# The 1/rms row of the first SwiGLU, formed between the halves of the second gate/up pair instead of ahead of both

## The chip, the cores and the metric

The kernel runs on one core of a Trainium2 chip, as one launch. The metric is device time in microseconds (us) of that core, from runs of the whole program. The profile is one further execution of the same program, taken by the hardware profiler. Engines are named as the profile names them: PE (TensorE matmuls), PEld (its weight loads), DVE (VectorE), ACT (ScalarE), POOL (GpSimd), SP (SyncE, which issues most DMAs).

## The reference

One decoder layer on 512 tokens of width 1024, all in float32: a SwiGLU half step, a mixer with two groups of attention heads, a second SwiGLU half step, and a gated embedding. What the change touches is the first SwiGLU:

```
def rmsnorm(x, g):
    xf = x.astype(jnp.float32)
    y = xf * lax.rsqrt(jnp.mean(xf * xf, axis=-1, keepdims=True) + EPS)
    return (y * g.astype(jnp.float32)).astype(x.dtype)

def swiglu(x, wg, wu, wd):
    return (jax.nn.silu(x @ wg) * (x @ wu)) @ wd

h = h + 0.5 * swiglu(rmsnorm(h, ffn1_norm[i]), ffn1_wg[i], ffn1_wu[i], ffn1_wd[i])
```

The hidden width is 2816. 1/rms is one number per token, so it may be multiplied in before or after the products with Wg and Wu.

## The kernel before, in words

**Products.** Every float32 product is made of three matmuls: both operands are split into a rounded part `hi` and a rest `lo`, and hi x hi, hi x lo and lo x hi are added up in PSUM (`passes`, L459). A weight tile is loaded into a buffer `st` (3 of them), rounded on ACT into a buffer `hi` (4), and the rest is formed on DVE into a buffer `lo` (4), by `split` (L375).

**The first SwiGLU.** The hidden columns are worked in 11 pairs of 128-column blocks. The token axis stays in the free dimension: a gate or up product of one block is a PSUM tile of 128 hidden columns x 512 tokens, and 24 matmuls (8 blocks of the contraction x 3 passes). Pair 0 is done by `ffn_start` (L473): x arrives transposed and without 1/rms, and its four products fill two `gub` and two `acc` banks of PSUM. Pairs 1 and 2 are done by `gate_up` (L552), each as two halves (r = 0 and 1) of a gate and an up product, all in `gub` banks, of which there are four. Pairs 3 to 10 are done by `Blocks` (L1292) with a scheme of seven block products per pair; its operands on the x side, `x8_165` to `x8_170` and `k4_171`/`k4_172` in the listings below, are built by `x_operands` (L581) from four `pt` buffers, which the scheme's first weights then reuse. Some of these weights are sums that a DMA of POOL's queue adds into a `pt` buffer (`accum_op`), others sums made on DVE (`V.tensor_add`). `down` (L618) multiplies the hidden values with Wd.

**The row.** Because x has no 1/rms in it, every product of pairs 0 to 2 and every operand of `x_operands` is multiplied by a row: 1/rms of the 512 tokens, the same on all 128 partitions. `rms_rows` (L514) makes it. For each of four blocks of 128 tokens:

```
            nc.scalar.activation(junk, h[t], AF.Square, accum_out=ss)
            r = self.rstd(ss, D)
            rb = self.w2()[:, :P]
            nc.vector.tensor_copy(rb, r.to_broadcast([P, P]))
            nc.tensor.transpose(ps[:, t * P:(t + 1) * P], rb, self.ident)
```

that is, a square with a sum on ACT, two small operations on POOL (`rstd`, L391), a copy on DVE and a transpose on PE; then ACT copies the PSUM tile into the row. `hidden` (L529) multiplies a pair's products by the row on DVE, which also frees their PSUM banks, and applies silu on ACT and a product on DVE.

**What sets the order.** Every instruction is first recorded in program order with an estimated cost (`Plan`, L59). `issue` (L214) then replays the recording as a simulation: it takes, for each engine, the earliest operation that can start, among a window of 440 operations after the oldest one not yet placed, with buffers given out in order. What comes out is emitted as each engine's fixed order. So code that is recorded in another order can give other orders on every engine. The recorded costs and the window are the same before and after.

Of the kernel before, what the change touches and what calls it, by code (L numbers as in the profile page):

```python
# [308 lines left out]
class Layer:  # L309
# [239 lines left out]
        nc.vector.tensor_sub(lo, a, hi.bitcast(F32))  # L549
        return hi, lo  # L550

    def gate_up(self, p, xT, quarters, ahead=None):  # L552

        nc = self.nc
        out = []
        for r in range(2):
            pair = []
            for g in range(2):
                w = self.st()
                for c in range(2):  # L560
                    nc.sync.dma_start(w[:, 512 * c:512 * c + 512], quarters[p, r, c, :, 512 * g:512 * g + 512])
                w = self.split(w.rearrange("p (k c) -> p k c", k=NK), NK, P)
                if ahead and r == g == 1:
                    ahead()
                ps = self.gub()
                for k in range(NK):
                    for i, (a, b) in enumerate(self.passes(w, [y[:, k % 2] for y in xT[k // 2]])):
                        nc.tensor.matmul(ps, lhsT=a[:, k, :], rhs=b, start=(k == 0 and i == 0),
                                         stop=(k == NK - 1 and i == 2))
                pair.append(ps)  # L570
            out.append(pair)
        return out


# [71 lines left out]
                if half == 1 and final:  # L646
                    on_token(t)

    def ffn(self, h, xT, quarters, wd, on_token, started=None, row=None):


        n = FF // (2 * P)
        classic = CLASSIC + (started is not None)
        raw, acts = [], []
        blocks = Blocks(self, range(classic, n), quarters)

        def parts():
            while raw:
                acts.append(self.hidden_parts(raw.pop(0)))
        X = None  # L660
        for p in range(n):
            if p < classic:
                first = p == classic - 1
                if first:
                    blocks.ahead(7, 0, 0)
                products = started if p == 0 and started else self.gate_up(
                    p, xT, quarters, (lambda: blocks.ahead(7, 3, 2)) if first else None)
                raw.append(self.hidden(products, row))
                if p == classic - 2:
                    X = self.x_operands(xT, row)  # L670
            else:
                i = 7 * (p - classic)
                end = i + 7 if p in (3, 7, n - 1) else len(blocks.seq)
                for j in range(7):
                    blocks.ahead(i + j + 7, min(i + j + 5, end), min(i + j + 3, end))
                    if j == 2:
                        parts()
                    blocks.product(i + j, X)
                raw.append(blocks.acts)
            if p in (3, 7, n - 1):  # L680
                parts()
                e = 7 * (p + 1 - classic)
                self.down(h, acts, p + 1 - len(acts), p == n - 1, wd, on_token, lambda: blocks.ahead(e + 7, e + 3, e + 2))
                acts = []
# [69 lines left out]
    def head_norm(self, E, src, dst, gain):  # L754
# [7 lines left out]
        else:  # L762
            E.tensor_tensor(sq, src, src, ALU.mult)
        nc.vector.tensor_reduce(ss, sq, axis=AX.X, op=ALU.add)
        r = self.rstd(ss, 64, n)
# [212 lines left out]
    def cmp_attention(self, A, t, g, o):  # L978
# [10 lines left out]
        m, rs = self.small(4), self.small(4)  # L989
        nc.vector.tensor_reduce(m, s, axis=AX.X, op=ALU.max)  # L990
        bc = lambda x: x[:, :, None].to_broadcast([P, 4, 32])
        nc.gpsimd.tensor_tensor(s, s, bc(m), ALU.subtract)
        nc.scalar.activation(s, s, AF.Exp)
        nc.vector.tensor_reduce(rs, s, axis=AX.X, op=ALU.add)
        nc.vector.reciprocal(rs, rs)
# [74 lines left out]
    def mix(self, xT, rs_in, o_nsa, o_fox, nsa_out):  # L1070
# [25 lines left out]
        def kv_project():  # L1096
# [4 lines left out]
            def kv_done(t, ps):  # L1101
# [8 lines left out]
                nc.scalar.activation(sq.rearrange("p (a h d) -> p a h d", a=2, h=2), uv[:, :, 0], AF.Square)  # L1110
                V.tensor_reduce(ss, sq.rearrange("p (n d) -> p n d", n=4), axis=AX.X, op=ALU.add)
                r = self.rstd(ss, 64, 4).rearrange("p (a h) -> p a h", a=2)
# [179 lines left out]
class Blocks:  # L1292
# [4 lines left out]
    def __init__(self, layer, pairs, quarters):  # L1297
        self.layer, self.quarters = layer, quarters
        self.seq = [(p, i) for p in pairs for i in self.ORDER]
        self.sums = self.loads = self.splits = 0  # L1300
        self.src, self.w = {}, {}

    def ahead(self, sums, loads, splits):

        L = self.layer
        nc = L.nc
        V, f = nc.vector, self.src

        def load(p, name, r, c, t):
            nc.sync.dma_start(t, self.quarters[p, r, c])  # L1310
            f[p, name] = t
        while self.sums < min(sums, len(self.seq)):
            p, i = self.seq[self.sums]
            if i in (7, 5):
                load(p, i, 1, 0, L.pt().bitcast(F32)[:, :1024])
                nc.gpsimd.dma_start(f[p, i], self.quarters[p, 0, 0] if i == 7 else self.quarters[p, 1, 1],
                                    accum_op=ALU.add)
            self.sums += 1
        while self.splits < min(splits, len(self.seq)):
            self.load_to(max(loads, self.splits + 1), load)  # L1320
            p, i = self.seq[self.splits]
            src = f[p, {6: 5, 3: 5}.get(i, i)]
            if i in (6, 3):
                V.tensor_add(src, src, f[p, 1 if i == 6 else 2])
            hi, lo = L.hi(), L.lo()
            nc.scalar.copy(hi, src)
            V.tensor_sub(lo, src, hi.bitcast(F32))
            self.w[p, i] = hi, lo
            self.splits += 1
        self.load_to(loads, load)  # L1330
# [53 lines left out]
def layer(ctx, tc, d, out, upto=99):  # L1384
    L = Layer(ctx, tc, d)
# [5 lines left out]
        nc.sync.dma_start(out[0, t * P:(t + 1) * P], h[t])  # L1391
    h = [L.k4() for t in range(NT)]
    xT, started = L.ffn_start(x, h, L.gcol["ffn1_norm"], d["first"])
    row = L.rms_rows(h)
    spill = [L.dram.tile([P, D], F32, name=f"spill{t}") for t in range(NT)]
    aT, a_r = [], []

    def to_mix(t):
# [3 lines left out]
            aT.append(L.new_xT())  # L1402
        a_r.append(L.norm_tok(t, h[t], None, aT[0], L.gcol["mix_norm"]))
        nc.sync.dma_start(spill[t], h[t])
    L.ffn(h, xT, d["quarters1"], d["ffn1_wd"][0], to_mix, started, row)
    if upto == 1:
        return nc.issue()
    L.mix_consts()
# [2 lines left out]
    h = []  # L1411
# [34 lines left out]
    xT = L.pairs_xT()  # L1446
# [108 lines left out]
```

## Time and profile before

| what | value |
|---|---|
| time, median of 3 runs | 1085.66 us (1085.31 to 1086.53) |
| the profiled execution, its own time | 1086.66 us |
| its span, first to last instruction | 1084.8 us |
| PE busy | 1068.4 us, 98% of the span |
| PEld, DVE, ACT, POOL busy | 89%, 71%, 53%, 17% |
| TensorE clock granted, mean | 1.000 |

The profiled execution lies 1.00 us above the median of the runs, and its span is 1.86 us shorter than its own time. All times inside the program are us from the span's start. The busy share of PE is high because matmuls overlap one another; what matters for this change is the first 100 us, and there what PE, ACT and DVE wait for. All helpers record their operations through one line (L306), so rows are told apart by their tiles: `gub` and `acc` are PSUM, `k` the 4 KB buffers (x, the x operands of pairs 0 to 2, hidden values), `w` the 2 KB ones (the row, the copies of 1/rms, the scaled products), `s` single columns.

### The profile page before, as it was taken

To read this page: it belongs to the slowest core of one execution; us is meant where nothing else is said; L and a number is where in the kernel's file an instruction comes from. 1 tells how busy PE (TensorE), PEld (TensorE's weight loads), DVE (VectorE), ACT (ScalarE), POOL (GpSimd) and SP (SyncE) were. 2 spreads that over 40 slices of the span, in tenths; PEclk is the share of its full clock that TensorE was granted. 3 is DMA by queue.
4 is the path that set the end of the run, shared out by engine and by line. 5 is a ranking of instruction groups with operands and counts; after the bars stand their busy time and mean duration, and the time that the engine had idled before them with its cause. 6 is when DMAs were issued, how large, how long until landed. Compare 5 with 4: busy or idle time off the path is not lost.

```text
span 1084.8 us, 17688 instructions
## 1 busy us (share of the span) xinstructions
PE 1068.4 (98%) x6721; PEld 962.8 (89%) x6721; DVE 768.4 (71%) x1320; ACT 580.2 (53%) x1116; POOL 184.2 (17%) x313
## 2 busy tenths in 40 slices
PE   9999999999999999999999999999999999999998
PEld 6789899988997878999999888889989998899887
DVE  5886378744774777989889786977537784487473
ACT  5544145522543768988888864645315552255352
POOL 0010000000000246554344610310000000000000
PEclk9999999999999999999999999999999999999999
DMA  8396356643444622302102241686535674333421
GB/s 280 125 232 200 97 136 184 189 130 100 118 110 131 216 70 73 86 7 60 43 18 75 76 158 52 220 222 170 173 97 145 185 185 130 103 109 120 153 109 66
DMA packets 76532, 139.79 MB, mean 129 GB/s; under 512 B 13744, under 2 KB 33712, under 8 KB 76192
## 3 DMA queue, kind: packets, MB, share of 16 engines
q1 hardware_dynamic: 71376, 120.76, 34.4%
q0 software_dynamic: 4928, 17.89, 9.4%
q8 instruction: 53, 0.87, 0.3%
q14 instruction: 31, 0.25, 0.1%
q10 hardware_dynamic: 144, 0.02, 0.0%
HBM read 132.23 MB, written 6.42 MB: 128 GB/s over the span
## 4 chain that ended last, share of the span: by engine, by line
PE 86%; DVE 4%; ACT 3%; POOL 3%; DMA 2%; issue 2%; SPq 0%; ACTq 0%; POOLq 0%; DVEq 0%
PE acc L306 53%; PE gub L306 33%; DVE k L306 1%; POOL s L306 1%; DVE lo L306 1%; ACT w L306 1%; DMA st<-in_quarters 1%; DMA st<-in_first 1%; POOL r L306 1%; ACT k L306 1%; POOL w L306 1%; DVE w L306 1%; DMA gq<-in_q_norm_nsa 1%; ACT hi L306 1%; SPq L306 0%
## 5 line engine op out<-in xcount | busy, mean ns | idle before, releaser
L306 PE MATMUL acc<-hi,k 128*128 128x512 f32 (+1 forms) x832 | 262.7, 389 | 1.5 <-ACT k L306 0.9
L306 ACT CAST hi<-st 128x1024 fp32r<-128x1024 f32 (+4 forms) x150 | 148.5, 991 | 179.7 <-PE acc L306 93.2
L306 DVE TENSOR_TENSOR lo<-st,hi 128x1024 fp32r<-128x1024 f32 (+4 forms) x150 | 172.2, 1150 | 65.6 <-ACT hi L306 65.2
L306 PE MATMUL acc<-hi,x 128*128 128x384 f32 (+3 forms) x720 | 199.5, 349 | 0.3 <-ACT hi L306 0.3
L306 PEld LDWEIGHTS acc<-hi,k 128*128 128x128 f32 x832 | 155.9, 188 | 32.6 <-ACT k L306 1.8
L306 PE MATMUL acc<-lo,k 128*128 128x512 f32 (+1 forms) x432 | 163.9, 383 | 0.6 <-DVE lo L306 0.6
L306 ACT CAST hi<-pt 128x1024 fp32r<-128x1024 f32 x68 | 71.4, 1049 | 159.1 <-PE acc L306 90.3
L306 PE MATMUL gub<-x,hi 128*128 128x256 f32 x816 | 147.5, 282 | 0.0
L306 PE MATMUL acc<-x,hi 128*128 128x256 f32 x816 | 147.3, 282 | 0.0
L306 DVE TENSOR_TENSOR lo<-pt,hi 128x1024 fp32r<-128x1024 f32 x68 | 83.2, 1223 | 79.6 <-ACT hi L306 79.6
L306 PE MATMUL gub<-k,hi 128*128 128x512 f32 (+1 forms) x560 | 138.6, 338 | 0.0
L306 PEld LDWEIGHTS acc<-hi,x 128*128 128x128 f32 x720 | 127.2, 189 | 11.0 <-ACT hi L306 0.4
L306 PE MATMUL acc<-lo,x 128*128 128x384 f32 (+3 forms) x360 | 125.0, 348 | 1.7 <-DVE lo L306 1.7
L306 PEld LDWEIGHTS gub<-x,hi 128*128 128x128 f32 x816 | 126.2, 189 | 0.5
L306 PEld LDWEIGHTS acc<-x,hi 128*128 128x128 f32 x816 | 125.7, 189 | 0.0
L306 PE MATMUL gub<-x,lo 128*128 128x256 f32 x408 | 115.3, 283 | 0.0
L306 PE MATMUL acc<-x,lo 128*128 128x256 f32 x408 | 115.3, 283 | 0.0
L306 POOL DMA_DIRECT2D pt<-in_quarters x34 | 29.9, 880 | 476.3 <-DMA pt<-in_quarters 284.8
L306 PEld LDWEIGHTS gub<-k,hi 128*128 128x128 f32 x560 | 96.3, 190 | 12.2 <-ACT hi L306 1.2
L306 PE MATMUL gub<-k,lo 128*128 128x512 f32 (+1 forms) x280 | 94.6, 338 | 0.4 <-DVE lo L306 0.4
L306 PEld LDWEIGHTS acc<-lo,k 128*128 128x128 f32 (+1 forms) x432 | 79.4, 184 | 15.7 <-DVE lo L306 0.9
L306 PEld LDWEIGHTS gub<-x,lo 128*128 128x128 f32 x408 | 76.9, 189 | 0.0
(163 smaller groups left out, 1716.0 us busy)
## 6 DMA issues: line engine op xcount, KB each, us to landing
st<-in_quarters SPq DMA_DIRECT2D x51, 512.0 KB, 3.5
st<-in_ffn_wd SPq DMA_DIRECT2D x44, 512.0 KB, 4.4
pt<-in_quarters SPq DMA_DIRECT2D x34, 512.0 KB, 4.5
pt<-in_quarters POOLq DMA_DIRECT2D x34, 512.0 KB, 6.9
st<-in_quarters SPq DMA_DIRECT2D x32, 256.0 KB, 4.9
st<-in_w_in SPq DMA_DIRECT2D x48, 128.0 KB, 2.3
st<-in_first SPq DMA_DIRECT2D x16, 256.0 KB, 4.0
st<-in_w_in SPq DMA_DIRECT2D x8, 512.0 KB
```

The lines of the kernel that those rows point to most:

```text
L306: getattr(getattr(self.nc, op.eng), m)(*a, **k)
```

## The change

`rms_rows` is no longer called before `ffn`. It is handed in as a function, and `gate_up` calls it in pair 1, after the recording of the first half (r = 0) and ahead of the second. `hidden` of pair 0 is recorded at that place too. The second SwiGLU has no such row and is recorded as before.

```
-    def gate_up(self, p, xT, quarters, ahead=None):
+    def gate_up(self, p, xT, quarters, ahead=None, mid=None):
...
             out.append(pair)
+            if r == 0 and mid:
+                mid()
         return out
...
-        X = None
+        X, row = None, None
+
+        def begun():
+            nonlocal row
+            row = rows()
+            raw.append(self.hidden(started, row))
         for p in range(n):
             if p < classic:
...
-                products = started if p == 0 and started else self.gate_up(
-                    p, xT, quarters, (lambda: blocks.ahead(7, 3, 2)) if first else None)
+                if p == 0 and started:
+                    continue
+                products = self.gate_up(p, xT, quarters, (lambda: blocks.ahead(7, 3, 2)) if first else None,
+                                        begun if p == 1 and started else None)
                 raw.append(self.hidden(products, row))
...
-    row = L.rms_rows(h)
...
-    L.ffn(h, xT, d["quarters1"], d["ffn1_wd"][0], to_mix, started, row)
+    L.ffn(h, xT, d["quarters1"], d["ffn1_wd"][0], to_mix, started, lambda: L.rms_rows(h))
```

Three places of the emitted order matter. Numbers behind a name tell buffers of one kind apart.

**PE, behind the last matmul of pair 0.** Before, the four transposes of the copies `w2_...` stand here, and then pair 1 begins (`gub_142`):

```order
L306 MATMUL acc_87<-k4_82,lo_111 128x512
L306 MATMUL acc_112<-ident_66,w2_116 128x128
L306 MATMUL acc_112<-ident_66,w2_120 128x128
L306 MATMUL acc_112<-ident_66,w2_124 128x128
L306 MATMUL acc_112<-ident_66,w2_128 128x128
L306 MATMUL gub_142<-k4_76,hi_140 128x512
L306 MATMUL gub_142<-k4_77,hi_140 128x512
```

Now 48 matmuls of pair 1's first half (into `gub_119` and `gub_123`) follow pair 0 directly, and the transposes stand behind them, ahead of the second half (`gub_150`):

```order
L306 MATMUL gub_123<-k4_82,lo_122 128x512
L306 MATMUL acc_124<-ident_66,w2_128 128x128
L306 MATMUL acc_124<-ident_66,w2_132 128x128
L306 MATMUL acc_124<-ident_66,w2_136 128x128
L306 MATMUL acc_124<-ident_66,w2_140 128x128
L306 MATMUL gub_150<-k4_76,hi_148 128x512
L306 MATMUL gub_150<-k4_77,hi_148 128x512
```

The four transposes moved 48 matmuls back on PE.

**ACT, at the same stretch** (`k4_70` to `k4_73` are x by tokens; the CASTs round weights). Before:

```order
L306 ACTIVATE k4_125,s1_126<-k4_73 128x1024
L306 CAST hi_140<-st_139 128x1024
L306 CAST hi_144<-st_143 128x1024
L306 CAST hi_148<-st_147 128x1024
L306 COPY w2_129<-acc_112 128x512
L306 ACT_TABLE_LOAD
L306 ACTIVATE w2_135<-w2_135 128x512
L306 ACTIVATE w2_137<-w2_137 128x512
L306 CAST hi_152<-st_151 128x1024
L306 CAST hi_176<-st_175 128x1024
L306 ACTIVATE w2_156<-w2_156 128x512
L306 CAST hi_180<-st_179 128x1024
```

Now:

```order
L306 ACTIVATE k4_137,s1_138<-k4_73 128x1024
L306 CAST hi_117<-st_116 128x1024
L306 CAST hi_121<-st_120 128x1024
L306 CAST hi_148<-st_147 128x1024
L306 CAST hi_152<-st_151 128x1024
L306 CAST hi_176<-st_175 128x1024
L306 CAST hi_180<-st_179 128x1024
L306 COPY w2_141<-acc_124 128x512
L306 ACT_TABLE_LOAD
L306 ACTIVATE w2_143<-w2_143 128x512
L306 ACTIVATE w2_145<-w2_145 128x512
L306 ACTIVATE w2_156<-w2_156 128x512
```

The four squares stay ahead of the first cast; the copy of the row (`w2_141`) went from behind the third cast to behind the sixth.

**DVE** (`w2_128` to `w2_140` are the copies of 1/rms). Before, the products of pair 0 are scaled behind the third `lo` (`lo_149`). Now:

```order
L306 COPY w2_140<-s1_139 128x128
L306 TENSOR_TENSOR lo_118<-st_116,hi_117 128x1024
L306 TENSOR_TENSOR lo_122<-st_120,hi_121 128x1024
L306 TENSOR_TENSOR lo_149<-st_147,hi_148 128x1024
L306 TENSOR_TENSOR lo_153<-st_151,hi_152 128x1024
L306 TENSOR_TENSOR lo_177<-st_175,hi_176 128x1024
L306 TENSOR_TENSOR lo_181<-st_179,hi_180 128x1024
L306 TENSOR_TENSOR w2_143<-gub_84,w2_141 128x512
```

The copies stay ahead of the first `lo`, and the first scaling (`w2_143`, which reads pair 0's bank `gub_84`) stands behind the sixth. Further on, where the first block products take their weights (`pt_173`, `pt_174`), the order on DVE is now this; the third of these rests, `lo_202<-pt_174,hi_202`, follows behind two more operations (`k4_196`, `k4_220`):

```order
L306 TENSOR_TENSOR lo_194<-pt_174,hi_193 128x1024
L306 TENSOR_TENSOR k4_218<-k4_142,k4_217 128x1024
L306 TENSOR_TENSOR w2_200<-gub_195,w2_141 128x512
L306 TENSOR_TENSOR pt_174<-pt_174,st_190 128x1024
```

Before, that third rest and the sum it needs (`pt_174`) stood ahead of `k4_218` and `w2_200`.

## Rows read from the trace of the kernel before

**Rows 1.** The page: its span, and the chain that ended last, by engine.

```profile
span 1084.8 us, 17688 instructions
...
PE 86%; DVE 4%; ACT 3%; POOL 3%; DMA 2%; issue 2%; SPq 0%; ACTq 0%; POOLq 0%; DVEq 0%
```

**Rows 2.** Windows: stretch, length, busy us of PE, PEld, DVE, ACT, POOL, clock, DMA.

```profile
25.00:30.00 5.00, 3.39 (x16) 2.44 (x14) 0.61 (x3) 3.26 (x7) 2.10 (x6) 1.00 0.62 238
...
50.00:100.00 50.00, 50.00 (x301) 44.83 (x300) 41.84 (x46) 24.55 (x30) 5.32 (x6) 1.00 0.85 226
...
200.00:300.00 100.00, 100.00 (x668) 92.49 (x667) 61.44 (x70) 38.47 (x49) 2.65 (x3) 1.00 0.44 128
```

**Rows 3.** Waits of PE, 0 to 130 us: total us, times, longest.

```profile
PE acc L306 <- DVE w L306: 3.3, 3, 1.2
PE gub L306 <- DVE lo L306: 0.4, 1, 0.4
```

**Rows 4.** Timeline of PE: start, us, instruction, count, idle time before and its releaser.

```profile
27.68 0.38 PE L306 MATMUL acc<-ident,w 128*128 128x128 f32 x2
29.21 0.33 PE L306 MATMUL acc<-ident,w 128*128 128x128 f32 x1 [1.16 <-DVE w L306]
30.45 0.33 PE L306 MATMUL acc<-ident,w 128*128 128x128 f32 x1 [0.90 <-DVE w L306]
...
31.62 0.50 PE L306 MATMUL gub<-k,lo 128*128 128x512 f32 x1 [0.38 <-DVE lo L306]
...
42.19 0.62 PE L306 MATMUL gub<-k,hi 128*128 128x512 f32 x2
...
74.83 0.40 PE L306 MATMUL gub<-x,hi 128*128 128x256 f32 x2
```

**Rows 5.** Timeline of ACT, 28 to 76 us.

```profile
28.07 1.06 ACT L306 ACTIVATE k<-k 128x1024 f32<-128x1024 f32 x1
...
29.12 3.17 ACT L306 CAST hi<-st 128x1024 fp32r<-128x1024 f32 x3
32.20 0.58 ACT L306 COPY w<-acc 128x512 f32<-128x512 f32 x1
32.79 1.28 ACT L306 ACT_TABLE_LOAD   x1
...
42.20 1.05 ACT L306 CAST hi<-st 128x1024 fp32r<-128x1024 f32 x1 [1.23 <-PE gub L306]
...
75.05 1.04 ACT L306 CAST k<-k 128x1024 fp32r<-128x1024 f32 x1
```

**Rows 6.** Timeline of DVE, 30 to 44 us.

```profile
30.16 0.23 DVE L306 COPY w<-s 128x128 f32<-128x128 f32 x1 [1.00 <-POOL s L306]
30.34 3.50 DVE L306 TENSOR_TENSOR lo<-st,hi 128x1024 fp32r<-128x1024 f32 x3
...
40.22 2.35 DVE L306 TENSOR_TENSOR pt<-pt,w 128x1024 f32<-128x1024 f32 x2
42.49 0.68 DVE L306 TENSOR_TENSOR w<-gub,w 128x512 f32<-128x512 f32 x1
43.09 1.22 DVE L306 TENSOR_TENSOR pt<-pt,w 128x1024 f32<-128x1024 f32 x1
```

**Rows 7.** The chain in order of time: start, us, what (two block products).

```profile
80.75 5.76 PE acc L306 x48
```

**Rows 8.** Timeline of the queues of SP and POOL: a load, and its addition.

```profile
55.27 0.33 SPq L306 DMA_DIRECT2D pt<-in_quarters  x1
...
60.32 0.88 POOL L306 DMA_DIRECT2D pt<-in_quarters  x1 [1.52 <-DMA pt<-in_quarters]
```

**Rows 9.** DMA issues at 60.3, 156.6 and 195.9 us: KB, us to landing.

```profile
pt<-in_quarters POOLq DMA_DIRECT2D x1, 512.0 KB, 9.5
...
pt<-in_quarters POOLq DMA_DIRECT2D x1, 512.0 KB, 7.5
...
pt<-in_quarters POOLq DMA_DIRECT2D x1, 512.0 KB, 5.2
```

More of the change, by code (lines that the diff above doesn't have):

```diff
@@ L647, in down, with ffn @@
                     on_token(t)
-    def ffn(self, h, xT, quarters, wd, on_token, started=None, row=None):
+    def ffn(self, h, xT, quarters, wd, on_token, started=None, rows=None):
         n = FF // (2 * P)
```

## The prediction

> **What bounds the kernel now.** I read the page first. Its chain [rows 1] says that 86% of the span is PE's own work: what stops PE costs time, what stops another engine only if PE then waits for it. The windows show where PE is ever short of work in this part: it has 3.39 of 5 us from 25 to 30 us, and all of it from 50 to 100 us and, far on, from 200 to 300 us [rows 2]. The list of PE's waits up to 130 us is therefore short [rows 3]: three waits for DVE's copies (one at the very start, the others below) and one for a rest `lo`.
>
> The timeline shows that place. Pair 0 ends about when the transposes begin at 27.68 us; the third transpose waits 1.16 us, the fourth 0.90 us, and pair 1 then 0.38 us for its first `lo`, at 31.62 us [rows 4]: 2.44 us of idle PE. It is what the change could win at most. From there PE runs without a gap: the second half of pair 1 begins at 42.19 us, the block products at 74.83 us [rows 4]. Six products lie between, so one takes (74.83 − 42.19) / 6 = 5.44 us.
>
> **The change, part by part.** Nothing is removed or added. The four squares, eight POOL operations, four copies, four transposes, the copy of the row and the table load are all still there; the first sixteen stay where they were, the last six move. POOL's queue is the same, and on SP's one weight load moves ahead of one into `pt`, which its own free buffer allows. So two questions: does the early gap close, and is the new place covered?
>
> *The early gap: 0.* The first cast of weights still stands behind the fourth square (28.07 us, the cast at 29.12 us [rows 5]), and the first `lo` still behind the fourth copy (30.16 us, `lo` at 30.34 us [rows 6]). That `lo`, not the transposes, is what PE waits for last, and it still ends at 31.56 us. Bounds: nothing won, or 2.44 us. I take 0, since neither queue's order changed ahead of it; and pair 1's second half still comes up at 42.19 us.
>
> *The new wait at 42.19 us: 2.9 us.* All four `gub` banks are then in use: two by pair 0, two by the first half. The next product needs `gub_84` scaled away, which needs the row, which needs the transposes. ACT's copy of the row stands behind the sixth cast, which needs a `hi` buffer that the first half holds to its end: before, this very cast starts at 42.20 us, released by PE [rows 5]. So:
> - the sixth cast, 42.20 to 43.25 us (1.05 us [rows 5]); the transposes (two took 0.38 us [rows 4]) and the row's copy (0.58 us [rows 5]) end by 43.9 us beside what follows;
> - the sixth `lo` on DVE, from 43.25 us. Its successor starts 1.135 us later: in [rows 6] two such operations and the step to the next take 42.49 − 40.22 = 2.27 us. So 44.38 us;
> - the first scaling, 0.68 us [rows 6], ends at 45.06 us, and PE starts about 0.06 us later, as behind the first `lo` (31.56 to 31.62 us): 45.12 us.
>
> PE is 45.12 − 42.19 = 2.9 us late. Lower bound: cast and `lo` not in the way, 42.19 + 0.76 + 0.58 + 0.68 + 0.06 = 44.27 us, that is 2.1 us. Upper bound: nothing overlaps, 0.76 + 1.05 + 0.58 + 1.22 + 0.68 + 0.06 = 4.4 us. I take 2.9 us because both queues' orders say who is in front. The table load (1.28 us [rows 5]) now follows the copy, to 45.2 us; only silu waits for it.
>
> *The delayed operands: 0.8 us.* What queued behind the row on DVE is late by more than PE is. From 44.38 us DVE has, up to the end of `x8_165`, 12 operations of the 512 form and 8 of the 1024 form; the small ones follow each other in 0.60 us (42.49 to 43.09 us [rows 6]): 44.38 + 7.2 + 9.1 = 60.7 us. Three large ones later, at about 64.2 us, `pt_161` is free and the second weight load of the blocks starts; before, it started at 55.27 us [rows 8]. It is 8.9 us late, PE only 2.9. POOL's addition followed after 60.32 − 55.27 = 5.05 us [rows 8], so now at 69.25 us. Additions took 9.5 us there, 7.5 us as the second of a pair and 5.2 us almost alone [rows 9]; the late one overlaps one other addition, so I take 7.5 us: landed at 76.75 us.
>
> From landing to the third rest, by the new orders: cast 1.05, rest 1.135, `k4_218` 1.135, `w2_200` 0.60, the sum 1.135, `k4_196` 0.60, `k4_220` 1.135, the rest 1.22: 8.0 us, so 84.8 us. A second chain gives almost the same: `k4_217`'s cast takes a buffer that x holds until the gate/up products end (it ran at 75.05 us, just behind 74.83 us [rows 4, 5]); now they end at 77.76 us, and 1.05 + 1.135 + 0.60 + 1.135 + 0.60 + 1.135 + 1.22 = 6.9 us later it is 84.7 us. PE wants that rest in its third block product: 77.76 us, plus 5.76 us for two products [rows 7], plus four matmuls that need only `hi` parts, 0.5 us: 84.0 us. So it waits 0.8 us. With an addition of 9.5 us it waits 2.8 us, with 5.2 us 0.7 us by the second chain. If ACT and DVE win a microsecond on their way, nothing: bounds 0 and 2.8 us.
>
> On the DMA I weighed a rule: the rows show 5.2 to 9.5 us for one such addition of 512 KB [rows 9]. The Trainium skill, page "DMA: Bandwidth & Descriptors", section "Anatomy of one DMA — SWDGE (gpsimd) path", fits 2.0 us plus the bytes over 436 GB/s, an estimate of 3.2 us here. By it the second chain alone would decide: 0.7 in place of 0.8 us. The trace does not agree with it for additions, so rows are used.
>
> *Afterwards: no recovery.* From 95 us the orders are the same, and PE has no idle time to give back (100 of 100 us from 200 to 300 us [rows 2]). Loads and casts wait for PE's buffers, so they shift along.
>
> **Sum.** 0 + 2.9 + 0.8 = 3.7 us. The profiled execution (1086.66 us; span 1084.8 us [rows 1]) would become 1090.4 us; it lies 1.00 us over the median of the runs, 1085.66 us, which becomes **1089.4 us**.
>
> **The rivals.** A measurement of this kernel can tell about 0.2%, 2.2 us, from no change.
> - *Only the first wait (0.12):* DVE and ACT catch up before the third block product, whose rest comes by 84.0 us. For it: it misses by only 0.8 us in my sum. Against: the second chain does not depend on DMA. 1085.66 + 2.9 = 1088.6 us.
> - *A late addition (0.10):* it takes 9.5 us as before [rows 9], or the fourth product's weights are late too. 2.9 + 2.8 = 5.7 us: 1091.4 us.
> - *Same (0.12):* the row is made without the sixth cast and `lo` in front, or what is late is made up: 2.1 us, 1087.8 us or less. For it: the row's inputs are ready since 30.4 us. Against: the cast at 42.20 us is released by PE [rows 5] and stands ahead of the row.
> - *Faster (0.04):* the other side. The transposes are out of the way, so the gap from 27.7 to 31.6 us closes (−2.44 us) while the new place stays covered: 1083.2 us. It needs the first `lo` to start by about 28 us; the fourth copy is in front of it at 30.16 us [rows 6]. A change that does nothing would count as same; the three orders exclude it.
> - *The clock (0.04):* PE's idle stretch at 42 us, unbroken for some 2.3 us, drops the granted clock. From 25 to 30 us PE was idle for 1.6 us in pieces and kept 1.00, the 2.4 GHz level [rows 2]; no row shows a longer break. If one 5.44 us product then ran at half speed: 5.4 us more, 1094.8 us. The Trainium skill, page "TensorE: Matmul & The Clock Gate", section "Part 1: The HAM clock gate (the "warmup" mystery)", says that an idle array falls to the lower of two clocks and leaves it only after sustained work. By that rule this rival holds if the break counts as idle; the trace neither shows nor excludes it.
> - *My forecast (0.58):* both waits, 3.4 to 5 us in all.
>
> **How the numbers follow.** Slower by over 0.2%: 0.58 + 0.12 + 0.10 + 0.04 = 0.84; within 0.2%: 0.12; faster: 0.04. The range leaves out the clock, the faster case and half of "same" (0.14), and takes in the bounds 2.1 and 5.7 us: 1087.6 to 1091.4 us.
>
> **What would show it.** In the new profile PE should still wait for a `lo` until about 31.6 us; the transposes should stand at 42.2 us with an idle stretch behind them to 45.1 us, released by DVE's scaling; the block products should begin near 77.8 us, with a wait for a rest near 84 us. ACT's copy of the row should start near 43.2 us, right behind a cast. I am wrong if PE starts pair 1 before 31 us, if the second half starts before 44 us, or if PE makes the time up after 100 us.

## The result, and the profile after

The change makes the kernel slower, and by more than I gave as the range: 1092.12 us median of 4 runs (1091.08 to 1094.3) against 1085.49 us of the kernel before beside them (1084.64 to 1086.53), a ratio of 1.0065 [1.0053, 1.0077], about 7 us. The forecast was 3.7 us. The same kernel, run again beside the last experiments, gave 1.0066 [1.0049, 1.0082]. The profiled execution of the changed kernel took 1092.39 us, with a span 5.8 us longer than before [rows 1].

The page of after, span and the chain that ended last by engine:

```profile
span 1090.6 us, 17693 instructions
...
PE 82%; DVE 5%; ACT 4%; DMA 3%; POOL 3%; issue 2%; SPq 1%; POOLq 0%; ACTq 0%; DVEq 0%
```

PE held 86% of the chain [rows 1] and now holds 82%: PE waits in more places. The windows of after, columns as in [rows 2]:

```profile
25.00:30.00 5.00, 4.01 (x17) 2.71 (x16) 2.46 (x5) 4.75 (x7) 1.93 (x5) 1.00 0.60 230
40.00:45.00 5.00, 2.67 (x10) 2.02 (x9) 3.93 (x6) 4.06 (x5) 0.00 (x0) 0.76 0.49 163
45.00:50.00 5.00, 5.00 (x22) 4.04 (x21) 3.82 (x6) 0.64 (x2) 0.00 (x0) 0.89 0.01 5
80.00:90.00 10.00, 8.13 (x52) 7.43 (x51) 10.00 (x12) 6.75 (x8) 0.97 (x2) 0.85 0.94 199
50.00:100.00 50.00, 48.13 (x277) 42.75 (x276) 43.16 (x45) 25.56 (x30) 4.43 (x5) 0.97 0.64 170
200.00:300.00 100.00, 100.00 (x668) 92.49 (x667) 61.94 (x71) 38.23 (x48) 4.39 (x5) 1.00 0.48 135
```

Two places are new. PE is busy 2.67 us of the 5 from 40 us and 8.13 of the 10 from 80 us. And the third number from the end, the granted clock, is 0.76, 0.89 and 0.85 there: in both places PE first stands idle and then works at a lower clock. Finer windows show the levels (from 44 to 46 us and from 88 to 90 us it is 0.50 too):

```profile
41.00:42.00 1.00, 0.00 (x0) 0.00 (x0) 0.93 (x1) 0.98 (x3) 0.00 (x0) 1.00 0.02 6
42.00:43.00 1.00, 0.05 (x1) 0.05 (x1) 1.00 (x3) 0.89 (x2) 0.00 (x0) 0.82 0.00 0
43.00:44.00 1.00, 1.00 (x3) 0.81 (x4) 1.00 (x2) 0.56 (x1) 0.00 (x0) 0.50 0.74 164
...
87.00:88.00 1.00, 1.00 (x7) 1.00 (x6) 1.00 (x3) 1.00 (x2) 0.00 (x0) 0.51 0.73 143
...
90.00:91.00 1.00, 1.00 (x8) 1.00 (x8) 1.00 (x2) 0.00 (x0) 0.00 (x0) 0.79 0.55 94
```

PE does nothing from 41 to 42 us, and the clock goes to 0.50 of full speed, the 1.2 GHz level, at about 42.6 us, just before PE starts again. It stays there until 46 us; the same level comes back from 87.0 to 90.4 us. PE's waits of after up to 130 us (total us, times, longest) say what it waited for:

```profile
PE gub L306 <- DVE w L306: 2.3, 1, 2.3
PE acc L306 <- ACT hi L306: 1.6, 2, 1.1
PE acc L306 <- DVE w L306: 1.2, 1, 1.2
PE gub L306 <- DVE lo L306: 0.7, 1, 0.7
PE gub L306 <- ACT hi L306: 0.3, 1, 0.3
PE acc L306 <- DVE lo L306: 0.3, 1, 0.3
```

The 1.2 us for `w` is the one at the very start, one of the three of [rows 3]. The 2.3 us is the scaling `w` that frees a `gub` bank; the `hi` and `lo` of `acc` are the third block product. PE's timeline of after, as [rows 4]:

```profile
28.05 0.73 PE L306 MATMUL gub<-k,hi 128*128 128x512 f32 x2 [0.31 <-ACT hi L306]
29.46 0.50 PE L306 MATMUL gub<-k,lo 128*128 128x512 f32 x1 [0.67 <-DVE lo L306]
...
40.02 0.60 PE L306 MATMUL acc<-ident,w 128*128 128x128 f32 x4
42.95 1.22 PE L306 MATMUL gub<-k,hi 128*128 128x512 f32 x2 [2.33 <-DVE w L306]
...
77.17 0.40 PE L306 MATMUL gub<-x,hi 128*128 128x256 f32 x2
...
84.33 0.50 PE L306 MATMUL acc<-x,hi 128*128 128x256 f32 x2 [1.14 <-ACT hi L306]
85.28 0.51 PE L306 MATMUL acc<-x,hi 128*128 128x256 f32 x2 [0.45 <-ACT hi L306]
86.07 0.38 PE L306 MATMUL acc<-x,lo 128*128 128x256 f32 x1 [0.29 <-DVE lo L306]
...
92.90 0.40 PE L306 MATMUL gub<-x,hi 128*128 128x256 f32 x2
```

With these starts the two executions can be laid side by side, up to the fifth block product, which begins at 92.90 us here and at 86.34 us in the trace of before:

| step | before | after | difference |
|---|---|---|---|
| first half of pair 1 ends | 42.19 | 40.02 | −2.17 |
| from there to the second half's first matmul | 0 | 42.95 − 40.02 | +2.93 |
| from there to the first block product (six products) | 32.64 | 34.22 | +1.58 |
| from there to the third product's first `lo` in the order of after | 6.26 (5.76 + 0.5, as predicted) | 8.90 | +2.64 |
| from there to the fifth block product (44 matmuls) | 5.25 | 6.83 | +1.58 |
| sum | | | +6.56 = 92.90 − 86.34 |

The 6.26 us of before is the start of the fifth matmul of the third product (that product begins at 80.58 us there), since in before no `lo` was waited for. The 5.25 us is 44 matmuls of three per 0.358 us, the pace of PE before 83 us. The two waits make 5.57 us of this, the lower clock 3.16 us. The −2.17 us is not the change's. In both kernels the first `lo` matmul of pair 1 starts 3.55 us behind the start of the fourth square (28.07 to 31.62 us before [rows 4, 5]; 25.91 to 29.46 us here), and ACT waits for x to arrive before its squares. In the second profiled execution of the changed kernel (after_again) it ran at 26.73 us, and the first half ended at 42.47 us instead of 40.02 us, partly because the clock fell there (below). The order on the engines is the same in both. In before_rest, which keeps the row ahead of pair 1, that square ran at 26.24 us: the early arrival is not tied to the change.

ACT and DVE at the first place, as [rows 5, 6]:

```profile
39.99 1.05 ACT L306 CAST hi<-st 128x1024 fp32r<-128x1024 f32 x1 [3.07 <-PE gub L306]
40.94 0.58 ACT L306 COPY w<-acc 128x512 f32<-128x512 f32 x1
```

```profile
41.07 1.23 DVE L306 TENSOR_TENSOR lo<-st,hi 128x1024 fp32r<-128x1024 f32 x1 [2.89 <-ACT hi L306]
42.21 0.68 DVE L306 TENSOR_TENSOR w<-gub,w 128x512 f32<-128x512 f32 x1
...
50.17 0.69 DVE L306 TENSOR_TENSOR w<-gub,w 128x512 f32<-128x512 f32 x1 [1.35 <-PE gub L306]
```

Cast, `lo`, scaling, PE: exactly the row of steps that the prediction gave. The last line is new: with PE at half its clock, DVE waits 1.35 us for a product, so the lower clock delays DVE too. In after_again, where the clock held at that place, the same scaling waited for nothing. At the second place, the chain of after in order of time (start, us, what) reads:

```profile
69.52 8.38 DMA pt<-in_quarters
...
77.97 1.06 ACT hi L306
...
84.88 1.15 DVE lo L306
...
86.07 6.99 PE acc L306 x44
```

POOL's addition starts at 69.52 us (predicted 69.25) and lands 8.4 us later (predicted 7.5); the rest is ready by 86.03 us, 8.1 us behind that, where 8.0 were counted.

### The profile page after: what moved, and what is told of

Same layout as the page of the kernel before. It is cut to its first block, busy times and chain, and to the rows that moved or that the text cites. A ratio compares the mean times of both kernels' runs of the same rounds, so it can differ in the third digit from the quotient of the medians.

```text
span 1090.6 us, 17693 instructions
## 1 busy us (share of the span) xinstructions
PE 1071.8 (98%) x6721; PEld 965.3 (89%) x6721; DVE 768.1 (70%) x1320; ACT 580.0 (53%) x1116; POOL 183.4 (17%) x313
## 4 chain that ended last, share of the span: by engine, by line
PE 82%; DVE 5%; ACT 4%; DMA 3%; POOL 3%; issue 2%; SPq 1%; POOLq 0%; ACTq 0%; DVEq 0%
PE acc L306 51%; PE gub L306 31%; DVE k L306 2%; DVE lo L306 2%; POOL s L306 1%; ACT w L306 1%; ACT k L306 1%; ACT hi L306 1%; DVE w L306 1%; POOL w L306 1%; DMA st<-in_first 1%; DMA pt<-in_quarters 1%; POOL r L306 1%; SPq L306 1%; DMA st<-in_quarters 1%
## 5 line engine op out<-in xcount | busy, mean ns | idle before, releaser
L306 DVE TENSOR_TENSOR lo<-pt,hi 128x1024 fp32r<-128x1024 f32 x68 | 83.1, 1223 | 78.8 <-ACT hi L306 78.8
L306 PEld LDWEIGHTS acc<-x,lo 128*128 128x128 f32 x408 | 77.6, 191 | 0.5 <-DVE lo L306 0.5
```

Source lines behind the costliest of these rows:

```text
L306: getattr(getattr(self.nc, op.eng), m)(*a, **k)
```

## The experiments

The account to be tested, A in the expectations, is: the loss is two waits and the lower clock behind them. The first wait is for the row's scaling. The second is in series with it through the operands that DVE makes later. The clock falls because PE stood idle. The other letters are rivals, each told where it stands. Every ratio is to runs of the kernel before beside it; their medians were 1084.25 us for the first four rows, 1083.80 us for the next four and 1083.84 us for the last four.

| run | what it has | median, us | ratio to before [95%] |
|---|---|---|---|
| fill1 | after, PE kept busy in the first wait | 1090.64 | 1.0054 [1.0043, 1.0065] |
| fill2 | and ahead of the second | 1091.18 | 1.0058 [1.0046, 1.0070] |
| acc_bank | after, no bank to wait for at 40 us | 1091.18 | 1.0061 [1.0049, 1.0073] |
| mid_early | the row one product earlier | 1088.42 | 1.0034 [1.0024, 1.0043] |
| x_late | and x by tokens loaded later | 1083.95 | 1.0001 [0.9992, 1.0010] |
| rest_first | after, third rest ahead of the hidden values | 1089.31 | 1.0051 [1.0038, 1.0064] |
| mid_early_rest | mid_early with that order | 1084.81 | 1.0013 [1.0004, 1.0022] |
| x_late_rest | x_late with that order | 1081.91 | 0.9982 [0.9974, 0.9991] |
| after_again | the change as it is | 1090.75 | 1.0066 [1.0049, 1.0082] |
| fill_both | PE kept busy in both idle stretches up to 45 us | 1089.55 | 1.0052 [1.0039, 1.0066] |
| rest_fill_both | rest_first with that filling | 1087.10 | 1.0030 [1.0018, 1.0042] |
| before_rest | before with the order of rest_first | 1083.85 | 1.0001 [0.9992, 1.0011] |

**Filling the idle time.** `fill` records matmuls whose result nobody reads, in an `acc` bank; the kernel's own output stays as it is.

```
             row = rows()
+            self.fill(xT[0][0], 9)
             raw.append(self.hidden(started, row))
...
+                    if started is not None and p == classic and j == 2:
+                        self.fill(X[5][0].rearrange("p k c -> p (k c)")[:, None, :512], 10)
                     blocks.product(i + j, X)
```

The first addition alone is fill1; fill2 has both.

> The changed kernel with nine matmuls whose result nobody reads, between the transposes and the second half of pair 1. They stand in PE's idle stretch of 2.3 us. Theory A (the loss is a wait of 2.9 us at the second half, a clock at the lower level behind it for 1.6 us, a wait of 2.5 us at the third block product, and a lower clock behind that for 1.6 us): the clock stays 1.00 from 40 to 50 us, both PE and the DVE operations that wait for it come 1.4 to 1.6 us earlier, ratio to before 1.0050, about 1090.5 us. Rival B (the lower clock costs nothing, since the third block product waits for DVE in any case): PE waits 1.6 us longer there, ratio 1.0065, about 1092.1 us.

> As fill1, and ten more such matmuls ahead of the third block product of the first block pair. Theory A: the clock stays 1.00 at 87 to 91 us too, another 1.5 us: ratio 1.0035, about 1089.2 us; what is left is the two waits. Rival B: no difference to the changed kernel, 1.0065. Rival E (the filling matmuls delay the third product): slower than fill1.

The clock held where PE was kept busy, but the time came down little: 1.0054 and 1.0058, intervals that overlap that of after. For fill1 this lies near A's 1.0050 and does not exclude B; for fill2 A's 1.0035 is missed. The windows of fill1 tell why:

```profile
30.00:35.00 5.00, 4.44 (x12) 3.51 (x13) 2.78 (x3) 1.54 (x3) 0.00 (x0) 0.66 0.57 175
40.00:50.00 10.00, 9.76 (x45) 7.72 (x44) 6.25 (x11) 4.72 (x6) 0.00 (x0) 1.00 0.31 105
```

From 40 to 50 us the clock is 1.00, but it now falls from 30 to 35 us, behind the gap at pair 1's start, which was left as it is. In the profiles of fill1 and fill2 the clock did not fall at the third block product, so there the second filling had nothing to win. So this pair of runs could not give the clock's price; it shows that the clock can also fall behind another idle stretch.

**Another bank for the second half.** In acc_bank the second half's gate product goes into an `acc` bank, so it need not wait for the scaling.

```
-                ps = self.gub()
+                ps = self.accb() if mid and (r, g) == (1, 0) else self.gub()
```

> The changed kernel, but the first product of pair 1's second half goes to a bank of the other PSUM group, which is free, so it need not wait for the scaling of pair 0. Theory A with the waits in series through DVE: the wait at the second half goes (2.3 us, and the lower clock of 1.6 us behind it), but the operands on DVE still start at the same time, so the wait at the third block product grows by about as much: ratio 1.0045 to 1.0065. Rival C (the two waits add up independently): 1.0065 - 0.0036 = 1.0029, about 1088.6 us. If the first wait stays, it was not the bank.

1.0061, inside A's range, and C's 1.0029 falls: nothing is won. PE's timeline has no wait near 40 us any more, and these instead, at the first block products:

```profile
75.64 0.50 PE L306 MATMUL gub<-x,hi 128*128 128x256 f32 x2 [2.06 <-ACT hi L306]
...
78.17 0.79 PE L306 MATMUL gub<-x,hi 128*128 128x256 f32 x2 [2.02 <-ACT hi L306]
```

The chain of acc_bank shows what the weights waited for:

```profile
59.97 1.15 DVE x L306
...
61.14 5.23 DMA pt<-in_quarters
...
66.93 7.59 DMA pt<-in_quarters
...
74.55 0.02 ACT hi L306
```

DVE's operand `x`, late as in after, sets a `pt` buffer free; then come the load, POOL's addition and the cast. The clock follows there, and stays low longer than in after:

```profile
75.00:80.00 5.00, 2.33 (x10) 2.13 (x11) 3.08 (x4) 3.10 (x4) 0.00 (x0) 0.62 1.04 256
80.00:85.00 5.00, 5.00 (x33) 5.00 (x32) 5.00 (x5) 3.05 (x3) 1.75 (x2) 0.69 0.71 174
```

PE arrives earlier and waits longer: 4.1 us of idle time at the block products where after has 1.9 us, so the 2.3 us saved at the first wait come back here. The two waits are in series: taking the first away alone brings the second forward. Part of the 1.0061 is the lower clock, which held for 6.8 us in this profile.

**The row earlier.** In mid_early `mid()` is called one product sooner, behind the first gate product of pair 1; three of the four `gub` banks are then in use, and the fourth takes the next product.

```
                 pair.append(ps)
+                if r == g == 0 and mid:
+                    mid()
             out.append(pair)
-            if r == 0 and mid:
-                mid()
```

> The changed kernel, but the row is recorded one product earlier: behind the gate product of pair 1's first half, not behind its up product. Theory A: the transposes run at about 36.5 us, ACT copies the row at about 39 us, DVE scales pair 0 by 41 us, before a bank is wanted at 42 us: no wait there and no lower clock; the operands are about 4 us later than before instead of 10, so at most 1 us of wait at the third block product: ratio 1.0000 to 1.0015, about 1086 us. Rival D (any place inside pair 1 costs, since DVE cannot make up the operands in time): 1.0030 or more.

1.0034: A, which gave 1.0015 at most, is missed, and the time is D's. The first wait is gone, as A said; what A had too small is the wait of the second kind, here 1.82 us, with the clock at 0.72 from 80 to 85 us behind it:

```profile
81.44 0.39 PE L306 MATMUL acc<-x,lo 128*128 128x256 f32 x1 [1.82 <-DVE lo L306]
```

**Loading x later.** In x_late the loads of x by tokens go behind the weight loads of pair 1 recorded so far, since the row no longer needs them first. It is mid_early with this edit:

```
-            if k == 4:
-                for t in range(NT):
-                    nc.sync.dma_start(h[t], x[t * P:(t + 1) * P])
...
+        nc.after = (max(o.i for o in nc.ops if o.eng == "sync"),)
+        for t in range(NT):
+            nc.sync.dma_start(h[t], x[t * P:(t + 1) * P])
+        nc.after = ()
```

> mid_early, and the loads of x by tokens stand behind the weights of pair 1's first half on SP's queue instead of ahead of most of them; the casts of these weights then stand ahead of the squares on ACT. Theory A: pair 1 starts right behind pair 0, so the early idle stretch of about 2.4 us goes; the row still comes before the second half needs it; the wait at the third block product moves along with PE: 2.4 us less than mid_early, ratio 1.0012. Rival G (the operands start when they started before, so PE gives the gain back at the block products): as mid_early, 1.0034.

1.0001, as fast as before and better than A's 1.0012; G falls. The gap at pair 1's start, which the forecast gave 2.44 us at most, closes: from 25 to 35 us PE is busy throughout. The first casts no longer stand behind squares that wait for x. One wait of the second kind, 1.50 us at 79.18 us, remains, and the clock is 1.00 there.

**The third rest first.** In rest_first the splitting of the hidden values of pairs 0 to 2 (`k4_217` to `k4_220`) may be planned only behind the third rest.

```
+                    if j == 0:
+                        rest6 = blocks.rest
                     if j == 2:
+                        if started is not None and p == classic:
+                            self.nc.after = (rest6,)
                         parts()
+                        self.nc.after = ()
...
+            self.rest = len(nc.ops) - 1
```

> The changed kernel, with one part of the order of before restored: the splitting of pair 0 to 2's hidden values (k_217/k_218, k_219/k_220) is put behind the third rest of the block weights on DVE and ACT. Theory A (the third block product waits because its rest stands behind these on DVE): from the landing of the second addition it is 5.7 us instead of 8.0 us to that rest, so the wait of 2.5 us shrinks to under 0.5 us and the lower clock behind it goes: ratio 1.0030, about 1088.5 us, with the first wait of 2.9 us and its lower clock left. Rival F (the landing of the addition itself is too late): the wait stays over 1.5 us, ratio 1.0050 or more.

> The row one product earlier (mid_early, 1.0034) and the third rest ahead of the split hidden values. Theory A: the wait of 1.8 us at the third block product goes, with the lower clock behind it: ratio 1.0000 to 1.0010, 1084.3 to 1085.3 us, no different from before. Rival F: the wait stays above 1 us, 1.0020 or more.

> x_late and the third rest ahead of the split hidden values. Theory A: no early gap, no wait for the row, under 0.5 us at the third block product, clock 1.00: 2.4 us under before, ratio 0.9978, about 1082 us. Rival G: 1.0000.

rest_first came out at 1.0051, above what A gives and within the time of F, but not with F's wait of over 1.5 us. Its windows and PE's timeline:

```profile
45.00:50.00 5.00, 5.00 (x16) 3.93 (x15) 5.00 (x8) 1.28 (x3) 0.00 (x0) 0.66 0.26 97
```

```profile
44.41 0.73 PE L306 MATMUL gub<-k,hi 128*128 128x512 f32 x2 [2.33 <-DVE w L306]
86.01 0.39 PE L306 MATMUL acc<-x,lo 128*128 128x256 f32 x1 [0.76 <-DVE lo L306]
```

The wait at the third rest did shrink to 0.76 us and did not go elsewhere; but the clock fell behind the first one. mid_early_rest has neither wait in its profile and took 1.0013, near A's 1.0010; seven of its eleven runs had a mean clock of 1.000 and took 1084.4 us on average, three had 0.998 and took 1087.1 us, and what lowered it in those three stays open, as no trace shows them. x_late_rest is faster than both kernels, 0.9982 [0.9974, 0.9991], 2 us below before, as A gave within the interval. In its profile PE has no idle time from 25 to 110 us:

```profile
25.00:110.00 85.00, 85.00 (x458) 73.82 (x457) 65.40 (x74) 42.19 (x53) 8.28 (x14) 1.00 0.68 198
```

**The clock held.** The last four runs ask what the clock did in rest_first and what its share is. fill_both has 4 unread matmuls ahead of pair 1 beside the 9 of fill1; rest_fill_both joins that to rest_first; before_rest puts the same order on the kernel before.

```
+                if p == 1 and started:
+                    self.fill(xT[0][0], 4)
                 products = self.gate_up(
```

> The change as it is, on the chip of the next three kernels, as their measure. Both theories: 1.0065 of the kernel before, mean granted clock 0.996 to 0.998.

> The change with unread matmuls in both idle stretches up to 45 us: 4 ahead of pair 1 (0.9 us) and 9 between the row's transposes and the second half of pair 1 (2.0 us). The waits for DVE stay, PE is busy. Theory A (the granted clock falls because PE is idle, and accounts for what the time has over the two waits): clock 1.00 from 25 to 50 us and mean 1.000 in nearly all runs, the waits alone, 5.5 us, remain: 1.0050. Rival (the lower clock has another cause and comes also behind a busy PE): 1.0060 or more, mean clock 0.998 or less.

> The same with the third rest put ahead of the splitting of the hidden values, as in the run before. That run came out at 1.0051 where 1.0030 was expected, with the clock at 0.66 from 45 to 50 us. Theory A: its surplus was the lower clock alone; with it held, the first wait and less than 1 us at the third rest remain: 1.0030 to 1.0035. Rival F (putting the rest ahead only shifts the wait to other operands): 1.0045 or more.

> The kernel before with only the new order of the third rest: the row stays ahead of pair 1. It tells what the best version owes to the order and what to the row's new place. Theory A (before, PE does not wait for a rest in the block products, so their order is worth nothing): 1.0000. Rival (the order by itself wins): 0.9982, the ratio of the version with the late loads of x and this order.

fill_both measured 1.0052, the 1.0050 that A gives, but its interval reaches the rival's 1.0060, and two of its six runs had a mean clock of 0.998, so filling did not hold the clock in nearly all. In its profile the clock is 1.00 in every window from 20 to 50 us and from 70 to 95 us. Among its waits up to 130 us are:

```profile
PE acc L306 <- ACT hi L306: 1.3, 2, 0.9
...
PE acc L306 <- DVE lo L306: 0.3, 1, 0.3
PE gub L306 <- DVE w L306: 0.2, 1, 0.2
```

Of the 1.9 us of idle time that after has at the third block product 1.6 us are still there. The last row is 0.2 us because the filling takes the place of the idle time, not because DVE is sooner. The steps of the table above, read in this profile, give 2.92 us for the first wait (40.42 to 43.34 us) and 2.27 us for the second (76.16 to 84.69 us, less 6.26): 5.2 us with the clock at 1.00. rest_fill_both measured 1.0030, against 1.0051 for rest_first: with the clock held, the first wait and 0.76 us remain. So the surplus of rest_first goes with the clock, and the rival (a wait shifted elsewhere) falls. The two intervals just touch, but the runs of rest_first say the same by themselves: four had a mean clock of 0.998 and took 1089.7 us on average, one had 1.000 and took 1087.44 us.

before_rest measured 1.0001, but it is a weak test: in before the third rest already stood ahead of the hidden values' splitting on DVE (75.18 and 76.32 us), so the edit moves only operations behind that rest. What it leaves is that x_late_rest does not owe its 2 us to the order alone: it has the order of before at this place, and beside it the row's later place and the later loads.

How often the clock fell also speaks for A. A mean clock of 0.998 or less is seen in 5 of the 61 runs of the kernel before beside these experiments, in 9 of the 10 runs of the changed kernel, in none of the 5 of rest_fill_both and in none of the 11 of x_late_rest, whose PE has no idle stretch.

after_again shows how loose the tie between an idle stretch and the clock is:

```profile
30.00:35.00 5.00, 4.72 (x14) 3.73 (x15) 2.50 (x3) 1.72 (x2) 0.00 (x0) 0.66 0.65 181
...
40.00:45.00 5.00, 3.07 (x16) 2.35 (x14) 1.48 (x2) 2.54 (x3) 0.00 (x0) 1.00 0.33 105
45.00:50.00 5.00, 4.60 (x20) 3.80 (x21) 5.00 (x9) 2.17 (x4) 0.00 (x0) 1.00 0.36 105
```

The very same wait of 2.33 us, up to 45.40 us, is followed by a clock of 1.00 here; the fall came earlier, behind the gap at pair 1's start.

## Why the prediction was wrong

- *The early gap, 0: right.* The first `lo` still ends last and 3.55 us behind the fourth square, in both kernels. The 2.17 us by which it came sooner in this execution is x's arrival. By it two of the signs that I gave for being wrong appeared, pair 1 before 31 us (28.05 us) and its second half before 44 us (42.95 us), without the mechanism being wrong: from the first `lo` to the first half's end it is 10.57 us before and 10.56 us after. Times from the span's start were a poor sign, as x's arrival moves them.
- *The new wait, 2.9 us: right.* It measured 2.93 us in after, in after_again (42.47 to 45.40 us) and in rest_first (41.48 to 44.41 us), by the steps that were named; 2.9 us was the forecast. The transposes end beside the cast, and the `lo` in front decides.
- *The delayed operands, 0.8 us: right in mechanism, but this term failed in size.* The wait was at the third block product, and 2.64 us long, near the upper bound of 2.8 (2.2 to 2.3 us in after_again and fill_both, where the clock held ahead of it). Of the 1.84 us missing, the addition's 8.4 us in place of 7.5 and its start 0.27 us later make 1.15 us. PE came 0.59 us sooner than the 77.76 us that I took, at 77.17 us, and so waited longer. Together 1.74 us, and 0.1 us more on the way from landing to rest. That the addition began within 0.3 us of the forecast is luck: x came 2.17 us sooner, but from the first half's end to that addition it was 29.5 us (28.4 us in after_again) where my sum has 27.1 us, and 1.35 us of this is DVE's wait for the product at half clock. The first `hi` also came late, not only the rest: the four matmuls that I let run ahead waited as well. The 7.5 us came from [rows 9], between 5.2 and 9.5 with little to lean on; in the profiles of fill1, fill2, rest_first, after_again, fill_both and rest_fill_both this addition took 7.7 to 8.7 us.
- *No more than that: wrong, and this is the step that put the time outside the range.* I left the clock out of the sum and gave it 0.04, because 1.6 us of idle time in pieces kept 1.00 [rows 2]. That reason did not hold: an unbroken 2.33 us brought the fall in two of three profiles, and pieces of 1.0 to 1.4 and 0.7 us brought it in fill1, fill2 and after_again. The clock cost 1.58 us behind each wait in the profiled execution. With the mis-sized wait alone the sum would be 2.93 + 2.64 = 5.6 us, or 1091.2 us, still inside the range; it is what I priced as "a late addition", and I never added two rivals up. The rule that I cited from the Trainium skill, page "TensorE: Matmul & The Clock Gate", section "Part 1: The HAM clock gate (the "warmup" mystery)", says that an idle array falls to the lower clock; the rows of after agree, with 0.50 from 43 us, and those of after_again, with 1.00 behind the same idle stretch, do not. My size for it, one product at half speed or 5.4 us, was too large: a stretch at the lower level cost 1.6 us, and there were two of them.
- *No recovery: not contradicted.* PE is busy 100 of 100 us from 200 to 300 us, as before. The span is 5.8 us longer where 6.56 us had been lost by the fifth block product; no experiment tells whether the 0.8 us is made up or is the difference between two executions.

The sum with what was measured: the waits, 2.93 + 2.64 = 5.6 us, agree with fill_both, where 0.0052 of 1083.84 us is 5.6 us, though two runs of fill_both had the lower clock too. The clock's part in the medians is the rest, 0.0066 − 0.0052, or 1.5 us; the intervals of the two runs overlap, so its size there is rough. Runs of one and the same kernel give a second measure: those with a mean clock of 0.998 took 2 to 3 us longer than those with 1.000 (fill1 1091.8 against 1089.9 us, mid_early 1088.4 against 1086.4, after_again 1091.1 against 1087.8). One of the six executions of after_again had a mean clock of 1.000, and it took 1087.78 us, 3.9 us over before: the waits may be worth less than 5.6 us in some executions. That the clock has a part is shown by the rows, and by rest_first against rest_fill_both (1.0051 to 1.0030). The lower end of my range should have read 1087.8 us (1085.66 + 2.1), not 1087.6; that changes nothing here. The side of the forecast, slower, was right.

## What to carry to other kernels

A wait of 2 us on a saturated PE can cost more than its length, for the clock may fall behind it and stay low for some 3 us, which cost about 1.6 us here: put that into the sum, with a chance, wherever an idle stretch is new, in one piece or in several. Add rivals up where they can come together. Moving work off a gap helps only if what feeds the gap moves too: here the row's later place cost time until the loads of x went behind the weights and the row came one product earlier (1.0001), and it won 2 us only when the third rest went first as well (0.9982). And when one wait is taken away, look at which operands were made late by the same cause, as they are the next wait.

## What was not expected of the hardware

- The clock fell to 0.50 behind an idle stretch of 2.33 us in the profile of after and rest_first, and stayed at 1.00 behind the same 2.33 us in that of after_again. Behind the broken gap at pair 1's start it fell in the profiles of fill1, fill2 and after_again (0.66 from 30 to 35 us) and held in those of before, after and rest_first. What decides between them, no run here tells.
- The lower level went again by itself: it held from 42.6 to 46.1 us and from 87.0 to 90.4 us in after, with PE at work from 42.95 us on and all through the second, and from 76.2 to 83.1 us in acc_bank.
- x by tokens reached ACT at different times in executions of one and the same order: the fourth square ran at 25.91 and at 26.73 us.
